# Ten weight parts of the memory's keys and values multiplied as rounded part and remainder instead of as native float32

## The chip, the cores and the metric

The kernel runs on one core of a Trainium2 chip. The metric is the device time of one execution in microseconds (us); the median of several runs is given. The engines are TensorE (PE, with its weight loads as PEld), VectorE (DVE), ScalarE (ACT), GpSimd (POOL) and SyncE (SP), which issues the transfers from memory.

## The reference

A trunk of two layers on 256 tokens of width 1024, all in float32. Each layer adds three things to the residual stream h: a mixer (an input projection of 2368 columns, two causal convolutions, a gated position mixing, a group norm, an output projection), a cross attention of 4 heads over 256 memory tokens, and a feed-forward part (a dense SwiGLU of 2816 in layer 0, eight experts of 3584 of which each token takes two in layer 1). A last norm follows. What the change touches is the projection of the normalized memory to keys and values:

```python
q = (xn @ w_xq).reshape(bsz, s, X_HEADS, X_HEAD_DIM)
k, v = jnp.split(memn @ w_xkv, 2, axis=-1)
scores = jnp.einsum("bshd,bmhd->bhsm", q, k) * (X_HEAD_DIM ** -0.5)
```

w_xkv is 1024 x 2048 in each layer, so keys and values of one layer are 16 parts of 128 x 1024 weights.

## The kernel before

**Parts and chunks.** All weights come through one stream of parts, 128 partitions x 1024 columns in most cases, loaded two at a time as a chunk of 1 MB by SP (L172) into a ring of 21 buffers (R_BUFS). In each layer the stream gives the mixer's input weights (wa, wb, wc), the key parts kb0 to kb7 (128 key columns each), the value parts vb0 to vb5 (two for each head of 256 columns, heads 0 to 2), eight parts of the mixer's output projection (mo), the value parts vb6 and vb7 of head 3, then q and the output of the attention. In layer 1, kb0 comes before the mixer's weights, kb1 has a chunk of its own behind them, and kb2 to kb5 are loaded and split during the dense feed-forward part and kept (L425 to L434).

**Two ways to multiply.** A part is either split or full. A split part is rounded to float32r by ACT (hi, L198), DVE subtracts that from the part (lo, L199), and each product becomes three rounded ones (mm3, L219 to L222): hi by hi, and each hi with the other side's lo. The other side must be split as well: for keys and values that is `ms`, which `split_m` (L468) makes from the normalized memory `mt`, its lo by DVE at L475. A full part is used as it lies, with `mt` itself, in one native float32 product: L463 for keys, L492 for values. The string FULL (L62) says for each of the sixteen parts of a layer which it is: eight keys, vb0 to vb5, then vb6 and vb7. In layer 1 the entries 0 and 1 go to kb0 and kb1 (L430), and 2 to 5 are not used, since those parts are kept (L425).

**What sets the order.** The program is written out by hand: each engine works through its instructions in the order in which the code issues them. `Stream.get` (L206) hands out the next part and, before that, splits parts up to three ahead (SPLIT_AHEAD), as long as they lie within three chunks of the current one (SPLIT_BUFS):

```python
while self.ns < min(i + 1 + ahead, len(self.parts)) and self.parts[self.ns][0] < c0 + bufs:
    self.do_split()
```

So a part's copy and subtraction are issued with the product of the part three places before it. `do_split` allocates hi and lo for a whole chunk when it first meets a part of it that is not full, and issues the loads three chunks ahead. Where the mixer stands is set by ORDER (L52), one string for each layer:

```python
ORDER = ["L 13 s b k a 4 k 5 k m 8 g 11 r k k 41 k 68 k 30 x t k 183 v1000 v8 33",
         "7 b s a k k k 4 m g 23 k k r k 42 k 86 v 31 t 14 v4 66"]
```

Here k is the next key part (`k_block`, L448), v the next head of values (`v_head`, L477), x is `split_m`, and a number is that many taps of the convolutions on DVE (`pop`, L142; the taps are at L548). In layer 1 `split_m` runs in the dense feed-forward part. The other letters are the branches: b transposes the second convolution back (L671, PE at L675, product at L677), s and a are the norm of the gated part (its last line L633), m the position mixing (PE at L687), g the gate (L697), r the scaling of the two branches (`sc_bc`, ending at L664), t their transposes (L300). With each part of wc, taps are issued as well, one in layer 0 and two in layer 1 (TAPS). Behind ORDER come the transposes of the first convolution (L724), its norm on DVE, head 2 of the values (L734), then the output projection. Evictions of keys and values are split too (L272 on ACT, L273 on DVE).

Of the kernel before, what the change touches and what calls it, by code (L numbers as in the profile page):

```python
# [58 lines left out]
ATTEND = ["q0 q1 S0 q2 S1 T0 q3 O0 T1 S2 S3 O1.T2.T3.O2.O3.",  # L59
          "q0 q1 S0 q2 T0 S1 q3 T1 O0 S2 S3 O1..T2 T3.O2 O3.."]  # L60

FULL = ["1111111110001100", "0110001111101100"]  # L62
SPL = [(j * 512, min(512, FF - j * 512)) for j in range((FF + 511) // 512)]


# [19 lines left out]
def trunk(tc, x, xt_in, mem, mt_in, wa, wb, wc, wl0, wk1, wl1, wff, wmoe, cc, tk, moec, ident_d, gfin, out):  # L85
    nc = tc.nc
    PE, ACT, DVE, POOL = nc.tensor, nc.scalar, nc.vector, nc.gpsimd
    with contextlib.ExitStack() as c:
# [1327 lines left out]
        def seq(a, n, w, full=None):  # L1416
            full = full or (False,) * (n * a.shape[0])
            return [(a[i], w, full[i * n:(i + 1) * n]) for i in range(a.shape[0])]

        def group(l):  # L1420
            return seq(wa[l], 2, 1024) + seq(wb[l], 2, 3 * BW) + seq(wc[l], 2, 2 * CW)

        def rest(l, a):

            f = tuple(x == "1" for x in FULL[l])
            n = l * KEPT
            f = f[2 * (l + n):14] + (False,) * 8 + f[14:16] + (False,) * 16
            return seq(a[n:], 2, 1024, f)

        one = (FULL[1][0] == "1",), (FULL[1][1] == "1",)  # L1430
        st = Stream(group(0) + rest(0, wl0) + seq(wff, 2, 1024) + seq(wk1[0:1], 1, 1024, one[0]) + group(1)
# [191 lines left out]
```

## Time and profile before

| | |
|---|---|
| median of 3 runs | 1512.85 us (1511.56 to 1518.7) |
| the profiled execution | 1510.55 us |
| its span on the core | 1508.7 us |
| mean granted TensorE clock | 0.989 |
| HBM over the span | 303 GB/s |

The span is the time from the first to the last instruction in the trace; the profiled execution's own time has what lies around it as well. A timeline row has the start, the time that the row takes, the engine, the line, the operation, out<-in and the count, and in brackets the idle time before it and what ended that. Rows that follow each other with one line and operation are merged. The start-to-start distance of matmuls tells their price better than the time of one, since they are pipelined.

### The profile page before, as it was taken

What the parts mean: (1) busy time and instruction counts of PE and PEld (TensorE: products, weight loads), DVE (VectorE), ACT (ScalarE), POOL (GpSimd) and SP (SyncE); (2) the same over time, 40 slices, a digit from 0 to 9 for tenths busy, and PEclk for the clock granted to TensorE, in tenths of its full rate; (3) what the DMA queues carried; (4) which work ended last, traced back from release to release, by engine and by line L of the source; (5) the groups of instructions that cost most, each with busy time, mean ns of one, the idle gap of its engine ahead of it and who ended that gap; (6) DMA issues with size and microseconds to landing.
All of it is one profiled execution on the core that took longest, in us unless ns stands there. A gap on an engine that the chain in (4) does not pass through costs nothing.

```text
span 1508.7 us, 20807 instructions
## 1 busy us (share of the span) xinstructions
PE 1469.5 (97%) x7757; PEld 1270.9 (84%) x7757; DVE 1293.9 (86%) x1496; ACT 1043.2 (69%) x1224; POOL 7.9 (1%) x23
## 2 busy tenths in 40 slices
PE   8999999999999998999999999999999999999995
PEld 7998988888999897788887878888888888888884
DVE  7988777545698866889999999999999999999996
ACT  7547565434544554688887788887878887888884
POOL 0000000000000001000000000000000000000000
PEclk9999999999999998899999999999999999999998
DMA  9535464544542547399999999999999999999992
GB/s 363 236 112 195 156 247 159 210 178 156 178 178 116 195 168 307 124 376 401 421 381 421 360 403 413 416 386 411 366 397 414 411 392 386 390 403 415 421 421 86
DMA packets 65326, 459.04 MB, mean 304 GB/s; under 512 B 7232, under 2 KB 7744, under 8 KB 11840
## 3 DMA queue, kind: packets, MB, share of 16 engines
q1 hardware_dynamic: 65216, 457.62, 76.5%
q8 instruction: 63, 1.03, 0.3%
q14 instruction: 47, 0.39, 0.1%
HBM read 456.55 MB, written 1.05 MB: 303 GB/s over the span
## 4 chain that ended last, share of the span: by engine, by line
PE 90%; DVE 4%; issue 2%; ACT 2%; DMA 1%; POOL 0%; SPq 0%; DVEq 0%; ACTq 0%; POOLq 0%
PE mm L1204 31%; PE acc L1204 16%; PE mm L220 5%; PE mm L222 5%; PE mm L221 5%; PE mm L1227 3%; PE acc L221 3%; PE acc L222 3%; PE acc L220 3%; PE mm L463 3%; PE z L221 2%; PE z L222 2%; PE z L220 2%; DVE lo L199 2%; PE mm L1149 2%
## 5 line engine op out<-in xcount | busy, mean ns | idle before, releaser
L199 DVE TENSOR_TENSOR lo<-w,hi 128x2048 fp32r<-128x2048 f32 (+3 forms) x504 | 946.4, 1917 | 56.9 <-ACT hi L198 37.8
L198 ACT ACTIVATE hi<-w 128x2048 fp32r<-128x2048 f32 (+3 forms) x504 | 795.1, 1619 | 111.9 <-PE mm L1204 58.0
L1204 PE MATMUL mm<-hi,xg 128*128 128x512 f32 x1344 | 405.4, 393 | 1.6 <-ACT xg L278 1.2
L1204 PEld LDWEIGHTS mm<-hi,xg 128*128 128x128 f32 x1344 | 253.0, 189 | 53.7 <-ACT xg L278 1.4
L1204 PE MATMUL mm<-lo,xg 128*128 128x512 f32 x896 | 295.3, 391 | 0.0
L1204 PE MATMUL acc<-hi,hl 128*128 128x512 f32 x672 | 217.4, 398 | 0.0
L1204 PEld LDWEIGHTS mm<-lo,xg 128*128 128x128 f32 x896 | 168.8, 188 | 34.1
L1204 PE MATMUL acc<-lo,hl 128*128 128x512 f32 x448 | 157.7, 393 | 0.0
L1204 PEld LDWEIGHTS acc<-hi,hl 128*128 128x128 f32 x672 | 125.2, 189 | 24.4
L1204 PEld LDWEIGHTS acc<-lo,hl 128*128 128x128 f32 x448 | 84.8, 189 | 17.4
L220 PE MATMUL z<-hi,xt 128*128 128x320 f32 (+1 forms) x256 | 79.0, 308 | 7.0 <-ACT xt L338 7.0
L221 PE MATMUL z<-lo,xt 128*128 128x320 f32 (+1 forms) x256 | 77.9, 304 | 0.2 <-DVE lo L199 0.2
L222 PE MATMUL z<-hi,xt 128*128 128x320 f32 (+1 forms) x256 | 78.0, 304 | 0.0
L548 DVE SCALAR_TENSOR_TENSOR ca<-ca,cct 128x256 f32<-128x256 f32 x180 | 77.1, 482 | 0.2
L220 PE MATMUL mm<-hi,xt 128*128 128x512 f32 (+1 forms) x192 | 71.9, 375 | 0.0
L222 PE MATMUL mm<-hi,xt 128*128 128x512 f32 (+1 forms) x192 | 71.5, 372 | 0.0
L221 PE MATMUL mm<-lo,xt 128*128 128x512 f32 (+1 forms) x192 | 71.4, 372 | 0.0
L1227 PEld LDWEIGHTS mm<-twice,gu 128*128 128x128 f32 x448 | 58.3, 191 | 6.0 <-ACT gu L1217 2.1
L1227 PE MATMUL mm<-twice,gu 128*128 128x64 f32 x448 | 56.2, 268 | 2.0 <-ACT gu L1217 2.0
L220 PEld LDWEIGHTS z<-hi,xt 128*128 128x128 f32 x256 | 49.7, 194 | 7.2 <-ACT xt L338 7.0
L221 PEld LDWEIGHTS z<-lo,xt 128*128 128x128 f32 x256 | 49.6, 194 | 0.5 <-DVE lo L199 0.5
L222 PEld LDWEIGHTS z<-hi,xt 128*128 128x128 f32 x256 | 49.5, 193 | 0.0
(284 smaller groups left out, 1891.5 us busy)
## 6 DMA issues: line engine op xcount, KB each, us to landing
w<-in_wmoe_dram SPq DMA_DIRECT2D x336, 1024.0 KB, 8.0
w<-in_wl_dram SPq DMA_DIRECT2D x39, 1024.0 KB, 4.8
w<-in_wff_dram SPq DMA_DIRECT2D x33, 1024.0 KB, 4.8
w<-in_wb_dram SPq DMA_DIRECT2D x8, 960.0 KB, 8.9
w<-in_wa_dram SPq DMA_DIRECT2D x5, 1024.0 KB, 4.9
w<-in_wc_dram SPq DMA_DIRECT2D x8, 640.0 KB, 4.6
tk<-in_tk_dram SPq DMA_DIRECT2D x2, 1024.0 KB, 10.5
mt<-in_mem_t_dram SPq DMA_DIRECT2D x2, 1024.0 KB, 8.2
```

Of the source, the lines that this page charges most:

```text
L198: ACT.activation(hi[:, ws], r, AF.Copy)
L199: DVE.tensor_tensor(lo[:, ws], r, hi[:, ws].bitcast(F32), op=OP.subtract)
L220: PE.matmul(ps, ah, bh, start=start, stop=False)
L221: PE.matmul(ps, ah, bl, start=False, stop=False)
L222: PE.matmul(ps, al, bh, start=False, stop=stop)
L463: PE.matmul(self.kps[:, d, :], w[:, ks], self.mt[:, k, :], start=k == 0, stop=k == KC - 1)
L548: return lambda: DVE.scalar_tensor_tensor(dst, src[:, k:k + S], w, dst, op0=OP.mult, op1=OP.add)
L1149: PE.matmul(ps[:, j * n:(j + 1) * n], src(t)[:, kk], self.pg[:, t, :], start=t == 0, stop=t == NT - 1)
L1204: PE.matmul(out, a, w, start=first and i == 0, stop=last and i == len(ops) - 1)
L1227: PE.matmul(ps[:, f * n:(f + 1) * n], w, twice, start=True, stop=True)
```

## The change

Ten entries of FULL go from 1 to 0. In layer 0 the parts kb7, vb0, vb4 and vb5, and in layer 1 kb7, vb0, vb1, vb2, vb4 and vb5, are split and multiplied with `ms` in three rounded products. kb0 to kb6 of layer 0, and kb1 and kb6 of layer 1, stay native. Nothing else changes.

```diff
-FULL = ["1111111110001100", "0110001111101100"]
+FULL = ["1111111000000000", "0110001000000000"]
```

## Rows read from the trace of the kernel before

**Rows 1.** The page, part 1: busy time of each engine.
```profile
PE 1469.5 (97%) x7757; PEld 1270.9 (84%) x7757; DVE 1293.9 (86%) x1496; ACT 1043.2 (69%) x1224; POOL 7.9 (1%) x23
```
**Rows 2.** Table of stretches: length, then busy us of PE, PEld, DVE, ACT, POOL.
```profile
470.00:480.00 10.00, 10.00 (x48) 8.80 (x48) 9.83 (x32) 1.54 (x2) 0.00 (x0) 1.00 0.26 92
```
**Rows 3.** Waits of PE, 62 to 545 us (all): total, times, longest.
```profile
PE acc L221 <- DVE lo L199: 0.2, 1, 0.2
```
**Rows 4.** Timeline of PE in layer 1, rounded products left out.
```profile
461.20 2.34 PE L687 MATMUL mm<-cv,tk 128*128 128x64 f32 x20
469.19 7.07 PE L463 MATMUL mm<-mt,w 128*128 128x256 f32 x32
476.09 7.07 PE L492 MATMUL mm<-w,mt 128*128 128x256 f32 x32
```
**Rows 5.** Lines L463 and L492, whole span: count, least, median, greatest ns.
```profile
L463 PE MATMUL mm<-mt,w x176: 377/380/484, 65.3 to 475.9; 128*128 128x256 f32 x176
L492 PE MATMUL mm<-w,mt x128: 377/380/382, 96.4 to 497.8; 128*128 128x256 f32 x128
```
**Rows 6.** Timeline of PE in layer 0: first and last of 48 rounded products.
```profile
102.70 0.28 PE L220 MATMUL mm<-hi,ms 128*128 128x256 f32 x1
...
108.34 0.28 PE L222 MATMUL mm<-hi,ms 128*128 128x256 f32 x1
```
**Rows 7.** Groups by line and shape, 60 to 150 us: busy us, mean ns.
```profile
L199 DVE TENSOR_TENSOR lo<-w,hi 128x1024 fp32r<-128x1024 f32 x16 | 19.0, 1221 | 1.1 <-ACT hi L198 1.1
L198 ACT ACTIVATE hi<-w 128x1024 fp32r<-128x1024 f32 x17 | 17.5, 1061 | 0.0
```
**Rows 8.** Timeline of DVE in layer 0.
```profile
90.39 0.69 DVE L273 TENSOR_TENSOR k<-mm,k 128x512 fp32r<-128x512 f32 x1
90.99 1.52 DVE L548 SCALAR_TENSOR_TENSOR ca<-ca,cct 128x256 f32<-128x256 f32 x3
...
93.03 1.22 DVE L199 TENSOR_TENSOR lo<-w,hi 128x1024 fp32r<-128x1024 f32 x1
94.16 2.35 DVE L475 TENSOR_TENSOR ms<-mt,ms 128x1024 fp32r<-128x1024 f32 x2
```
**Rows 9.** Timeline of PE in layer 0: the last key part.
```profile
92.92 3.62 PE L463 MATMUL mm<-mt,w 128*128 128x256 f32 x16
```
**Rows 10.** Timeline of DVE in layer 1.
```profile
444.94 0.88 DVE L548 SCALAR_TENSOR_TENSOR ca<-ca,cct 128x256 f32<-128x256 f32 x2
...
449.29 1.66 DVE L548 SCALAR_TENSOR_TENSOR ca<-ca,cct 128x256 f32<-128x256 f32 x4
451.43 1.07 DVE L677 TENSOR_TENSOR y<-mm,y 128x320 f32<-128x320 f32 x2 [0.47 <-PE mm L675]
...
459.98 0.49 DVE L633 TENSOR_TENSOR cv<-cv,tk 128x320 f32<-128x320 f32 x1
...
462.03 0.69 DVE L273 TENSOR_TENSOR k<-mm,k 128x512 fp32r<-128x512 f32 x1 [0.95 <-ACT k L272]
...
478.91 1.56 DVE L664 TENSOR_TENSOR y<-y,t 128x640 f32<-128x640 f32 x2
```
**Rows 11.** Line L172, 443.5 to 444.1 us: the issue and its landing.
```profile
L172 SPq DMA_DIRECT2D w<-in_wl_dram x1: 328/328/328, 443.8 to 443.8; - x1
...
DMA to landing us min/median/max: 4.9/4.9/4.9
```
**Rows 12.** Timeline of layer 0: the output projection's fifth part.
```profile
127.89 0.19 PEld L221 LDWEIGHTS acc<-lo,xt 128*128 128x128 f32 x1 [0.21 <-DVE lo L199]
```
**Rows 13.** Stretches (granted clock behind POOL), timeline of PE, waits of PE.
```profile
624.30:634.70 10.40, 10.40 (x43) 9.63 (x43) 6.74 (x12) 4.65 (x12) 0.00 (x0) 0.51 0.23 95
1484.50:1488.00 3.50, 3.50 (x10) 2.73 (x9) 3.07 (x3) 0.40 (x1) 0.00 (x0) 0.51 0.01 2
...
623.64 6.38 PE L1149 MATMUL mm<-pg,h 128*128 128x64 f32 x32 [3.14 <-DVE pg L1134]
...
PE mm L1179 <- DVE y L273: 4.5, 5, 1.2
```

## The prediction, made before the change was run

> **What bounds the kernel now.** I read the busy shares of the page first: TensorE (PE) is busy 97% of the span, VectorE (DVE) 86%, ScalarE (ACT) 69% [rows 1]. These are averages, and the ten weight parts are all used in two short stretches, the second half of the mixer of layer 0 (62 to 116 us) and of layer 1 (447 to 500 us). So the next view is the table of stretches, cut there. In 470 to 480 us PE is busy 10.00 of 10.00 us, but DVE is busy 9.83 and ACT only 1.54 [rows 2]. The reader is to see that PE has no gap, and that DVE, which would get new work, has no gap either. The waits of PE say the same from the other side: between 62 and 545 us PE waited once, 0.2 us, for a remainder that DVE writes at L199 [rows 3]. PE is the bound, with DVE a few microseconds behind it: whatever is taken off PE is worth its own time, and whatever is put on DVE ahead of something that PE needs is a wait that does not exist today.
>
> **What it takes off PE.** A native product leaves two records each: 11 parts of 8 products give the 176 records of L463, 8 parts the 128 of L492 [rows 5]. From 469.19 to 476.09 us PE went through 32 records, two parts, so a native part costs 3.45 us; the next 32 end with the same figure [rows 4]. The three rounded products at L220 to L222 start every 0.120 us: 48 of them from 102.70 to 108.34 us [rows 6]. A split part has 24, so 2.88 us. Each of the ten parts saves PE 0.57 us, 5.7 us in all. The Trainium skill (FP8 and Floating Point Precision, "TensorE Precision Notes") states that true FP32 takes 4 passes; were the three rounded products one pass each, an estimate from that would be a quarter of the part, 0.86 us, and 8.6 us for the ten (the sum below would come out 2 us lower). The rows show less, 0.57, and the rows decide.
>
> **What it adds.** Ten more copies at L198 on ACT, 1.06 us each, and ten more subtractions at L199 on DVE, 1.22 us each [rows 7] (1.13 from start to start, 93.03 to 94.16 us [rows 8]). ACT's 10.6 us I cost at nothing: it is the least busy engine in these stretches [rows 2]; were that cover gone, each copy would delay its subtraction by up to 1.06 us. No transfer is added. Five chunks that had no rounded tiles (in both layers the one with kb6 and kb7 and the one of head 2, in layer 1 the one of head 0) now take two buffers of the ring each, so later weight loads find a free buffer later. No row prices this: the lower end is nothing, since such loads were issued many microseconds ahead of use, the upper end some 5 us, the time of one load [rows 11]. I take nothing, as no wait of PE in rows 3 is for a load.
>
> The subtractions are issued three parts ahead and stand in DVE's queue in program order. So for each one I ask where in that queue it lands, and what PE needs next from behind it.
>
> **Layer 0, last key part (kb7).** Today it is multiplied with mt itself and begins at 92.92 us [rows 9]. Split, it needs ms, the remainder of the memory, which DVE writes at L475 from 94.16 us, 2.35 us for two halves [rows 8]. Today nothing needs ms before vb1. Now two new subtractions are queued ahead of it: kb7's after the first L273 (90.39 us), vb0's after the three taps at 90.99 us. The first half of ms then begins at 94.16 + 2 x 1.13 = 96.4 and ends near 97.6 us. PE can do one product at 92.92 and then stands until 97.6: a wait of 4.6 us. From then kb7 and vb0 save 0.57 each. Parts vb4 and vb5 (head 2) save 1.15 more, which I count as nothing: four output parts later PE already waits for a remainder, [0.21 <-DVE lo L199] at 127.89 us [rows 12], behind a chain of DVE that starts when the convolution is transposed and does not move with head 2. Layer 0: 4.6 - 1.15 = **+3.45 us**.
>
> **Layer 1, kb7.** Its subtraction is issued with the last part of wc. The load that brings it is issued at 443.8 us and lands 4.9 us later, at 448.7 [rows 11]; the copy takes 1.06, so DVE can subtract from 449.8 to 450.95. In DVE's queue the subtraction stands behind six of the fifteen taps that run from 444.94 us (two for each of the three parts before it); a tap takes 0.40 us, four of them 1.66 with the tail [rows 10], so DVE is there at about 447.3 and stands. The nine taps behind it now end at 450.95 + 9 x 0.40 = 454.5 instead of 450.95. The chain b, s, a that starts at L677 today at 451.43 [rows 10] starts 3.1 us later. PE works on kb1 to kb3 meanwhile and needs the end of that chain at L687, at 461.20 us [rows 4]; L633 ended at 460.47 [rows 10], 0.7 us earlier, so PE waits 3.1 - 0.7 = **2.4 us**.
>
> **Layer 1, vb0 and vb1.** vb0's subtraction is issued at kb1 and goes into DVE ahead of the taps and of r. vb1's is issued at kb6, and in the order string r stands before that, so it comes behind L664, which today ends at 478.91 + 1.56 = 480.5 [rows 10]. With the 3.1 us from kb7, 1.13 from vb0, and 0.95 of DVE's idle time (at 462.03 [rows 10]) used up, L664 ends at 483.7 and vb1's remainder is ready at 484.9. PE reaches head 0 at 476.09 [rows 4] + 2.4 - 0.57 = 477.9, does vb0 for the first token tile (12 products, 1.4 us) and needs vb1 at 479.4: a wait of **5.5 us**. What of L664's own reader, the transposes after head 0? They come after the wait and are ready. Savings that count: kb7, vb0, vb1, vb2, 2.3 us, and some 0.5 of head 2's 1.15, since in this layer the remainder four parts on has that much slack. Layer 1: 2.4 + 5.5 - 2.8 = **+5.1 us**.
>
> **The clock.** After a wait of 3.14 us for pg, PE began again at 623.64 and its granted clock was 0.51, the 1.2 GHz level, through 624.3 to 634.7 us; a shorter dip stands at 1484.5 to 1488.0 (0.51); behind the waits for y at L1179, the longest 1.2 us, I found no fall [rows 13]. Two new waits of 4.6 and 5.5 us are longer than 3.14, so I expect a fall behind each. What it costs is half of the low stretch: 1.7 us by the short one, 5.1 by the long one, none if the clock holds. I take 2.2, near the short one: as at 1484 us dense products follow at once, while after 623.64 us L1149's small ones did. Two falls: **+4.4 us**. The Trainium skill (TensorE: Matmul & The Clock Gate, "Why this matters for your kernels") likewise warns that idle gaps between bursts of matmuls return the array to half rate; the trace agrees with the 3.14 us gap, and this is the rule that speaks against the change.
>
> **Sum.** Waits 4.6 + 2.4 + 5.5 = 12.5, savings that count 4.0, clock 4.4: 12.9 us longer. From 545 us on the experts' stage keeps PE the bound, with its loads issued only as buffers come free, so I let all of it pass to the end. The profiled execution took 1510.55 us (span 1508.7), which makes 1523.5; the median of the runs, 1512.85, is 2.3 above it, so on the median 1525.8, given as **1526**. A measurement of this kernel tells some 0.5% (7.6 us) from no change.
>
> **Rivals.** (a) *Not slower.* The subtractions are ready in time and PE's saving stands: 4.0 to 5.7 us, 1507 to 1509. Its place is the remainder of ms in layer 0 and of vb1 in layer 1; it decides if DVE gets to them before 92.9 and 479.4 us. For it: rows 3, almost no wait today. Against it: DVE is at 9.83 of 10 us in front of the second point [rows 2], and rows 8 leave no gap before the first. Even the full 5.7 stays within 0.5%. Chance 0.12.
> (b) *One wait only*, because kb7's load in layer 1 or the place of vb1's subtraction is not as I read it. With layer 0 alone and one short dip it is 3.45 - 2.8 + 1.7 = 2.4, so 1515; with the 2.4 of L687 and 2 us at vb1 left, 6.8, so 1520. Chance 0.15.
> (c) *Both waits, the clock holds*: + 8.5, 1521. Against it stands the fall after 3.14 us. Chance 0.13.
> (d) *Long dips or late loads*: two dips of 5.1 and up to 5 us for a load that waits for the ring: 12.5 - 4.0 + 10.2 = 18.7, to 1532, and to 1537 with the load. Chance 0.15. That the lookahead turns out to split nothing new, so that nothing changes, gets 0.02, since L463 has 176 records today and must have 16 x 9 = 144.
> The forecast itself, both waits with short dips, has 0.43.
>
> **Range.** 1515 to 1534 takes in the forecast, (c), most of (b) and most of (d); left out are (a) and the far end of (d). Over 0.5% slower means above 1520.4: the forecast, (c), (d), 0.71 together. Within 0.5% are (a), (b) and nothing-changes: 0.29, of which I give 0.04 to over 0.5% faster, which needs more than the whole saving of PE.
>
> **What would show it.** L463 with 144 records (9 parts), L492 with none; L198 and L199 with 514 each. Step by step: PE waiting at L221 for ms (L475) near 93 us for 4 to 5 us; DVE waiting for hi (L198) near 447 us, L687 starting near 463.6; PE waiting for lo (L199) near 479 us for about 5 us; the granted clock below 1 behind the first and third. I am wrong if PE's gaps there stay under 1 us, if the waits are there but the clock is 1.00, or if the wait is for a load instead.

## The result and the profile after

The changed kernel takes **1531.71 us** (median of 6 runs, 1527.27 to 1532.82), beside 1514.59 us for six runs of the kernel before (1511.56 to 1518.7). The ratio is 1.0108, with a 95% interval of 1.0086 to 1.0131, so the kernel is slower by over 0.5%. The execution that was profiled took 1532.82 us (span 1531.0, mean granted clock 0.979), the highest of its six; that of before, 1510.55, lies below all six of its own. The two spans are 22.3 us apart, more than the medians (17.1), and that difference has to be explained too.

First the counts. From the page of the changed kernel, part 1, and then the groups of part 5 and the row of line L463 (they answer to [rows 1, 5]):

```profile
PE 1476.7 (96%) x7837; PEld 1279.5 (84%) x7837; DVE 1305.5 (85%) x1506; ACT 1053.4 (69%) x1234; POOL 7.9 (1%) x23
...
L199 DVE TENSOR_TENSOR lo<-w,hi 128x2048 fp32r<-128x2048 f32 (+3 forms) x514 | 958.4, 1903 | 63.3 <-ACT hi L198 44.8
L198 ACT ACTIVATE hi<-w 128x2048 fp32r<-128x2048 f32 (+3 forms) x514 | 804.7, 1607 | 119.3 <-PE mm L1204 56.7
...
L463 PE MATMUL mm<-mt,w x144: 377/379/483, 65.7 to 481.3; 128*128 128x256 f32 x144
```

L463 has 144 records and L492 none: the ten parts are split. DVE has 11.6 us more to do and ACT 10.2, about ten times the prices of [rows 7]. PE's busy time went up by 7.2 us although its work went down. The clock does that: at half speed the same product counts twice.

Next the waits of PE from 62 to 560 us, the view of [rows 3], where before there was one row of 0.2 us (columns: total, times, longest):

```profile
PE mm L221 <- DVE lo L199: 4.9, 1, 4.9
PE mm L221 <- DVE ms L475: 4.5, 1, 4.5
PE mm L675 <- DVE cb L548: 2.3, 1, 2.3
PE mm L300 <- DVE y L664: 0.5, 1, 0.5
PE acc L221 <- DVE lo L199: 0.4, 2, 0.2
```

Three new waits hold 11.7 us. The first to come in time is that for ms, in layer 0. PE's timeline of the changed kernel, the first product of kb7, the second behind the wait, the last, and the start of vb0:

```profile
93.21 0.36 PE L220 MATMUL mm<-ms,hi 128*128 128x256 f32 x1
98.08 0.58 PE L221 MATMUL mm<-ms,hi 128*128 128x256 f32 x1 [4.50 <-DVE ms L475]
...
102.94 0.41 PE L222 MATMUL mm<-ms,lo 128*128 128x256 f32 x1
103.15 0.41 PE L220 MATMUL mm<-hi,ms 128*128 128x256 f32 x1
```

And DVE's timeline of the same stretch, to hold against [rows 8]:

```profile
91.37 1.22 DVE L199 TENSOR_TENSOR lo<-w,hi 128x1024 fp32r<-128x1024 f32 x1
92.50 1.52 DVE L548 SCALAR_TENSOR_TENSOR ca<-ca,cct 128x256 f32<-128x256 f32 x3
93.94 1.22 DVE L199 TENSOR_TENSOR lo<-w,hi 128x1024 fp32r<-128x1024 f32 x1
95.07 0.69 DVE L273 TENSOR_TENSOR k<-mm,k 128x512 fp32r<-128x512 f32 x1
95.67 1.22 DVE L199 TENSOR_TENSOR lo<-w,hi 128x1024 fp32r<-128x1024 f32 x1
96.80 2.35 DVE L475 TENSOR_TENSOR ms<-mt,ms 128x1024 fp32r<-128x1024 f32 x2
```

Two subtractions that did not exist before (91.37 and 93.94) now stand ahead of ms, which begins at 96.80 instead of 94.16. DVE has no gap: it is late because it has more to do. kb7 on PE took 103.15 - 93.21 = 9.94 us. Its 24 products cost 2.88 [rows 6] and the wait 4.50, so 2.56 are left, and those are the clock: the products behind the wait start every 0.21 us (102.94 to 103.15), not every 0.120.

In layer 1 the load of kb7 comes first. DVE of the changed kernel, rows that answer to [rows 10]:

```profile
456.27 1.23 DVE L199 TENSOR_TENSOR lo<-w,hi 128x1024 fp32r<-128x1024 f32 x1 [2.51 <-ACT hi L198]
457.41 0.88 DVE L548 SCALAR_TENSOR_TENSOR ca<-ca,cct 128x256 f32<-128x256 f32 x2
458.20 1.26 DVE L548 SCALAR_TENSOR_TENSOR cb<-cb,cct 64x256 f32<-64x256 f32 x3
...
460.97 0.88 DVE L677 TENSOR_TENSOR y<-mm,y 128x320 f32<-128x320 f32 x2
...
488.21 1.56 DVE L664 TENSOR_TENSOR y<-y,t 128x640 f32<-128x640 f32 x2
489.69 1.22 DVE L199 TENSOR_TENSOR lo<-w,hi 128x1024 fp32r<-128x1024 f32 x1
```

DVE stood 2.51 us for the copy of a weight part that was still on its way, and the taps of cb at 458.20, queued behind that subtraction, were late. PE needs them at L675. PE's timeline in layer 1 has that wait, then L687 without one, then head 0:

```profile
459.61 1.19 PE L675 MATMUL mm<-ident,cb 128*128 128x128 f32 x6 [2.29 <-DVE cb L548]
...
470.03 2.34 PE L687 MATMUL mm<-cv,tk 128*128 128x64 f32 x20
...
484.34 0.28 PE L220 MATMUL mm<-hi,ms 128*128 128x256 f32 x1
...
490.96 0.58 PE L221 MATMUL mm<-lo,ms 128*128 128x256 f32 x1 [4.90 <-DVE lo L199]
...
497.46 1.25 PE L300 MATMUL mm<-ident,y 128*128 128x128 f32 x10
```

At 490.96 PE goes on when the remainder of vb1 is there, which DVE could only begin at 489.69, behind L664. The head took 497.46 - 484.34 = 13.12 us: 48 products at 0.120 are 5.76, the wait is 4.90, and 2.46 are the clock.

The table of stretches of the changed kernel says the same of the clock (the figure behind POOL; 1.00 is the 2.4 GHz level, 0.5 the 1.2 GHz one). The stretches are those behind the wait for ms, around the wait at L675, and behind the wait for vb1's remainder:

```profile
96.00:103.20 7.20, 5.12 (x24) 5.12 (x25) 6.25 (x9) 0.00 (x0) 0.00 (x0) 0.54 0.10 41
452.00:459.00 7.00, 5.33 (x37) 5.06 (x35) 4.49 (x11) 3.79 (x6) 0.00 (x0) 1.00 0.98 415
459.00:465.00 6.00, 5.39 (x29) 4.54 (x30) 5.86 (x22) 4.31 (x23) 0.00 (x0) 1.00 0.51 194
490.00:497.40 7.40, 6.44 (x35) 6.44 (x36) 5.79 (x7) 0.00 (x0) 0.00 (x0) 0.60 0.00 0
```

**Where the 22.3 us lie.** I follow landmarks through both traces; their rows in PE's timeline, two of the kernel before and one of the changed kernel (its L675 of layer 1 stands above):

```profile
450.81 1.16 PE L675 MATMUL mm<-ident,cb 128*128 128x128 f32 x6
...
587.53 0.96 PE L969 MATMUL mm<-mct,xf 128*128 128x8 f32 x8
```

```profile
601.44 0.96 PE L969 MATMUL mm<-mct,xf 128*128 128x8 f32 x8
```

The first L675 of layer 0, ahead of all that the change touches, starts at 64.23 us before and 64.60 after (0.4 of unequal start). L675 of layer 1 starts at 450.81 and 459.61; its wait of 2.29 taken off, layer 0 has cost 6.1 us. The first router product of layer 1 (L969) starts at 587.53 and 601.44, so from the first L675 to it ("the front" from here on) it was 523.3 us and is 536.8: **13.5 us more, 6.1 in layer 0 and 7.4 in layer 1**. Behind L969 the change touches nothing, yet the rest of the span takes 921.2 us before and 929.6 after. Those 8.4 us are a question for the experiments.

### The profile page after: what moved, and what is told of

The parts are those of the page before. It is cut to its first block, busy times and chain, and to the rows that moved or that the text cites. A ratio compares the mean times of both kernels' runs of the same rounds, so it can differ in the third digit from the quotient of the medians.

```text
span 1531.0 us, 20992 instructions
## 1 busy us (share of the span) xinstructions
PE 1476.7 (96%) x7837; PEld 1279.5 (84%) x7837; DVE 1305.5 (85%) x1506; ACT 1053.4 (69%) x1234; POOL 7.9 (1%) x23
## 4 chain that ended last, share of the span: by engine, by line
PE 84%; DVE 10%; issue 2%; ACT 2%; DMA 1%; POOL 0%; SPq 0%; DVEq 0%; ACTq 0%; POOLq 0%
PE mm L1204 30%; PE acc L1204 16%; PE mm L221 5%; PE mm L222 5%; PE mm L220 5%; DVE lo L199 3%; PE mm L1227 3%; PE acc L221 3%; PE acc L222 3%; PE acc L220 3%; DVE ca L548 2%; PE mm L1149 2%; PE z L221 2%; PE z L222 2%; PE z L220 2%
## 5 line engine op out<-in xcount | busy, mean ns | idle before, releaser
L199 DVE TENSOR_TENSOR lo<-w,hi 128x2048 fp32r<-128x2048 f32 (+3 forms) x514 | 958.4, 1903 | 63.3 <-ACT hi L198 44.8
L198 ACT ACTIVATE hi<-w 128x2048 fp32r<-128x2048 f32 (+3 forms) x514 | 804.7, 1607 | 119.3 <-PE mm L1204 56.7
```

Source lines behind the costliest of these rows:

```text
L198: ACT.activation(hi[:, ws], r, AF.Copy)
L199: DVE.tensor_tensor(lo[:, ws], r, hi[:, ws].bitcast(F32), op=OP.subtract)
```

## The experiments

My theory: three of the ten parts cost all of it, because DVE's queue delivers something too late: ms behind kb7 of layer 0, the taps of cb behind kb7 of layer 1 (whose load DVE stands for), and the remainder of vb1 of layer 1 behind L664. The clock falls behind the two long waits, and the other seven parts gain a little or nothing. Rivals: every part costs its share (of buffers, of loads, of DVE); or the clock alone costs it, by chance; or a better place in the order would have given the gain. All runs start from the changed kernel. The front is the profile's L969 less its first L675, 523.3 in the kernel before; the rest is the span less L969. Each ratio is against runs of the kernel before made alongside (14 of them for the first four rows, 18 for the next four); a row marked "one" is a single execution and has no ratio.

| run | median us (range) | ratio to before, 95% | front | rest |
|---|---|---|---|---|
| kb7 of layer 0 native | 1522.68 (1518.49 to 1525.26) | 1.0052 [1.0028, 1.0076] | 530.5 | 921.4 |
| vb1 of layer 1 native | 1526.56 (1522.44 to 1527.38) | 1.0080 [1.0056, 1.0104] | 532.0 | 923.5 |
| kb7 of layer 1 native | 1529.49 (1528.58 to 1531.02) | 1.0100 [1.0075, 1.0125] | 532.3 | 929.5 |
| all three native, seven split | 1514.38 (1511.61 to 1517.29) | 0.9991 [0.9974, 1.0008] | 521.7 | 923.6 |
| waits filled with products | 1524.84 (1520.7 to 1527.55) | 1.0056 [1.0037, 1.0075] | 534.9 | 926.5 |
| layer 0: ms earlier | 1527.32 (1524.35 to 1529.05) | 1.0067 [1.0046, 1.0088] | 532.9 | 929.2 |
| both orders changed | 1525.49 (1524.49 to 1527.46) | 1.0063 [1.0043, 1.0082] | 530.1 | 928.5 |
| both orders, kb7 of layer 1 native | 1520.3 (1514.83 to 1523.44) | 1.0025 [1.0011, 1.0040] | 527.6 | 920.3 |
| before, once more | 1516.09 (one) | | 523.2 | 925.8 |
| before, a third time | 1519.15 (one) | | 523.2 | 929.8 |
| changed kernel, once more | 1527.17 (one) | | 537.5 | 923.2 |
| only three split | 1509.41 (one) | | 521.6 | 921.1 |

**Which parts carry it.** Four kernels that give parts back:

```diff
-FULL = ["1111111000000000", "0110001000000000"]
+FULL = ["1111111100000000", "0110001000000000"]
```

> The changed kernel with one part put back: kb7 of layer 0 is native again, nine parts stay split. Theory (the cost is three waits of PE on DVE's queue and the clock that falls behind two of them): the 4.5 us wait for ms (L475) is gone, so is the half-speed stretch near 97 us (about 2.8 us), and 0.57 us of PE comes back; the first router product (L969, at 601.4 us in the changed kernel) starts about 6.7 us earlier, near 594.7; the waits at L675 and for vb1 in layer 1 stay at 2.3 and 4.9 us. Rival (the cost comes from the buffers and loads that every split part takes, in equal shares): L969 moves by a tenth of 13.9, 1.4 us. Rival (most of the difference is clock stretches of the experts' stage that come by chance): L969 hardly moves.

```diff
-FULL = ["1111111000000000", "0110001000000000"]
+FULL = ["1111111000000000", "0110001001000000"]
```

> The changed kernel with vb1 of layer 1 native again, nine parts split. Theory: the wait of 4.9 us for vb1's remainder (L199) behind L664 is gone and the half-speed stretch near 489 us (about 2.5 us) with it, against 0.57 us more of PE: L969 about 6.8 us earlier, near 594.6; the waits in layer 0 (4.5 us) and at L675 (2.3 us) stay. A smaller wait may come up at vb2's or vb3's remainder, which stand behind it in DVE's queue, under 1 us. Rival of equal shares: 1.4 us.

```diff
-FULL = ["1111111000000000", "0110001000000000"]
+FULL = ["1111111000000000", "0110001100000000"]
```

> The changed kernel with kb7 of layer 1 native again, nine parts split. Theory: DVE no longer stands for the load of kb7, so the 2.3 us wait of PE at L675 is gone; DVE's chain to L664 comes 3.1 us earlier and PE 2.4 - 0.57 us earlier, so the wait for vb1 stays, near 3.6 us, and the clock still falls behind it: L969 2 to 4 us earlier, near 598. Rival of equal shares: 1.4 us. Rival (the 2.3 us at L675 come from the taps alone, not from kb7's subtraction): the wait at L675 stays.

```diff
-FULL = ["1111111000000000", "0110001000000000"]
+FULL = ["1111111100000000", "0110001101000000"]
```

> The changed kernel with those three parts native again (kb7 of both layers, vb1 of layer 1), seven parts split. Theory: no wait of PE over 0.6 us between 62 and 560 us, no half-speed stretch before the router; L969 near the 587.5 us of the kernel before, less about 0.57 x 4 us that count of the seven, so 585 to 587.5, and the time the same as before or up to 2 us shorter. Rival of equal shares: seven tenths of the cost stay, L969 near 597.

Each native part took its own wait away and left the other two. With kb7 of layer 0 native the wait for ms is gone and the front is 6.3 us shorter than the 536.8 of the changed kernel; vb1 gives 4.8, kb7 of layer 1 4.5. The second had been expected some 2 us lower: behind the wait at L675, 2.17 us there, the clock now fell, which it had not done in the first profile of the changed kernel. Each gain is read from one profile and holds what the clock did in it, which differs by some 2 us between profiles (see the account of the clock below). The three gains add up to 15.6, and all three together gave 15.1; that they agree so closely is in part luck. What PE still waited for in that kernel, with seven parts split:

```profile
PE mm L300 <- DVE y L664: 0.5, 1, 0.5
PE acc L221 <- DVE lo L199: 0.4, 2, 0.2
```

Its front is 1.6 us *shorter* than before the change, and the time is that of before (0.9991). So seven of the ten parts cost nothing, nor do the buffers of the three chunks that take rounded tiles for them (the two chunks of kb6 and kb7 are all native again here): equal shares are refuted. The tables of stretches show how little room there is. First the kernel before, from L687 to L724, then the kernel with seven split parts in the same part of the work:

```profile
461.00:491.00 30.00, 30.00 (x192) 27.90 (x191) 24.87 (x63) 11.26 (x42) 0.00 (x0) 1.00 0.10 37
```

```profile
461.70:491.00 29.30, 29.30 (x212) 28.02 (x211) 29.09 (x68) 14.30 (x45) 0.00 (x0) 1.00 0.21 73
```

DVE's busy time (third figure with a count) goes from 24.87 of 30 us to 29.09 of 29.3. The four subtractions of vb0, vb2, vb4 and vb5 (1.13 us each) took the room that DVE had: some 0.2 us are left.

**How much of it is the clock.** The edit adds products that nobody reads, 38 ahead of kb7 in layer 0 and 41 ahead of vb1 in layer 1, so that PE works where it stood. Nothing is left out; the lines behind move by one to nine.

```diff
+                if self.l == 0 and i == KC - 1:
+                    z = mm("fill")
+                    for _ in range(FILL[0]):
+                        PE.matmul(z[:, 0:S], w[0][:, 0:P], self.ms.hi(0), start=True, stop=True)
...
+                        if self.l == 1 and hd == 0 and t == 0 and k == 4:
+                            z = mm("fill")
+                            for _ in range(FILL[1]):
+                                PE.matmul(z[:, 0:S], self.ms.hi(0, tok(0)), parts[0][0][:, 0:S], start=True, stop=True)
```

> The changed kernel, all ten parts split, with matmuls added whose results nobody reads: 38 of 128x256 ahead of kb7 in layer 0 and 41 between vb0 and vb1 in layer 1, 0.12 us each, on operands that are ready. They lie inside the two waits (4.5 and 4.9 us). Theory: DVE is as late as before, so the waits are filled, not shortened, and what is saved is the clock alone: no half-speed stretch near 97 and 489 us, L969 about 5.3 us earlier than in the changed kernel (601.4), near 596. Rival (the falls of the clock are not caused by PE standing still): the half-speed stretches stay and L969 stays at 601 or comes later.

The table of stretches of that kernel, behind the two filled waits and behind L684 (L675 in the other kernels):

```profile
97.00:104.00 7.00, 7.00 (x59) 6.86 (x58) 7.00 (x11) 2.49 (x3) 0.00 (x0) 1.00 0.30 101
457.00:464.00 7.00, 7.00 (x20) 5.07 (x20) 6.78 (x27) 3.52 (x22) 0.00 (x0) 0.53 0.34 135
490.00:498.00 8.00, 8.00 (x70) 8.00 (x69) 7.42 (x11) 2.48 (x7) 0.00 (x0) 1.00 0.17 51
```

Where PE was kept busy the clock stayed at 1.00, in both places: the 2.56 and 2.46 us belong to the idle time of PE. The remainders were hardly earlier for it (ms begins at 96.56 us and vb1's subtraction at 489.50; 96.80 and 489.69 in the changed kernel), so the waits' own time stayed, now filled with products. The front came out at 534.9 and not some 5 us below the changed kernel, because the clock fell at 457 us instead, behind a wait of 2.1 us that I had not filled. By the row above that fall cost some 3.3 us (7.00 us at 0.53). Of the 11.6 us by which this front is still longer than that of the kernel before, some 8 are then left with the clock at 1.00 behind both long waits: the rival that the clock alone makes the difference is refuted.

**Whether the order could be mended.** In layer 0 ms goes ahead of the two parts, at the price of later taps:

```diff
-ORDER = ["L 13 s b k a 4 k 5 k m 8 g 11 r k k 41 k 68 k 30 x t k 183 v1000 v8 33",
+ORDER = ["L 13 s b k a 4 k 5 k m 8 x g 2 r k k k k t k v1000 v8 33",
```

> The changed kernel, all ten parts split, with layer 0's order changed: the split of the memory (x) stands ahead of the gate (g), six taps ahead of r fewer, and the taps that are left come in the middle of head 0. Theory: the place in DVE's queue is what costs, not the amount of work: the wait for ms (4.5 us) and the half-speed stretch near 97 us are gone, with at most 1 us of new waits, L969 near 594.5. Layer 1 as in the changed kernel (waits of 2.3 and 4.9 us). Rival (DVE simply has too much to do in this stretch): the wait moves to the transposes of the first convolution (L724), which need all taps, and L969 stays within 2 us of 601.4.

The wait for ms and the fall behind it are gone, and kb7 and vb0 bring their saving: L724 of layer 0 starts 43.1 us after the first L675, before the change 44.2 (108.46 - 64.23). L969 still came 3.4 us later than expected (597.9 against 594.5). L300 waits 1.1 us for y instead of 0.5, and the wait for vb1's remainder is 0.5 us shorter than in the changed kernel; what is left is the price of a fall of the clock behind L675 of layer 1, which is seen in the 1.88 us of its row:

```profile
454.17 1.88 PE L675 MATMUL mm<-ident,cb 128*128 128x128 f32 x6 [2.12 <-DVE cb L548]
```

In layer 1 the next kernel moves r, the taps and head 0 as well, so that vb1's subtraction comes ahead of them:

```diff
-         "7 b s a k k k 4 m g 23 k k r k 42 k 86 v 31 t 14 v4 66"]
+         "7 b s a k k k m g 10 k k r k k v10 t v1000 66"]
```

> As the run before, with layer 1's order changed too: 10 taps ahead of r instead of 27, the rest in the middle of heads 0 and 1, all ten parts split. Theory: r and with it vb1's remainder come about 5 us earlier in DVE's queue, so the wait for vb1 falls from 4.9 us to under 1 and the half-speed stretch near 489 us goes; the 2.3 us at L675 stay; a wait of 1 to 3 us for the taps may come up at L724 of layer 1. L969 near 588, the time within 3 us of the kernel before. Rival (DVE has too much to do in layer 1): the 4.9 us come back at L724, L969 near 594.

Its row of L675 has the same wait ahead of it and takes 1.19 us, not 1.88: here the clock held.

```profile
454.28 1.19 PE L675 MATMUL mm<-ident,cb 128*128 128x128 f32 x6 [2.17 <-DVE cb L548]
```

Still the front was a miss, 530.1 us; L969 came at 595.1, near the 594 of the rival. Its waits of PE from 62 to 560 us:

```profile
PE mm L724 <- DVE ca L548: 4.8, 2, 3.4
PE mm L675 <- DVE cb L548: 2.2, 1, 2.2
PE mm L300 <- DVE y L664: 1.1, 1, 1.1
...
PE mm L221 <- DVE lo L199: 0.2, 1, 0.2
```

The wait for vb1's remainder shrank from 4.9 to 0.2 us, and L724 now waits 4.8 us for the taps that were put behind it. To see whether kb7's subtraction is what is too much, the next kernel has the same orders and kb7 of layer 1 native:

```diff
-FULL = ["1111111000000000", "0110001000000000"]
+FULL = ["1111111000000000", "0110001100000000"]
```

> As the run before, with kb7 of layer 1 native, nine parts split. Theory: the 2.3 us at L675 are gone as well, and no wait of PE over 1 us is left between 62 and 560 us; of the 9 x 0.57 us of PE some 3 to 4 us count, so L969 is at 584 to 586.5, 1 to 3.5 us ahead of the kernel before, and the time 0 to 4 us under it, hardly to be told from no change. Rival: a wait at L724 of 2 us or more, L969 at 587.5 or later.

A miss again, on the rival's side: L969 came at 592.9. The wait at L675 is gone, but PE's timeline at L724 shows:

```profile
490.11 0.27 PE L724 MATMUL mm<-ident,ca 128*128 128x128 f32 x1
493.60 0.47 PE L724 MATMUL mm<-ident,ca 128*128 128x128 f32 x1 [3.22 <-DVE ca L548]
495.56 1.11 PE L724 MATMUL mm<-ident,ca 128*128 128x128 f32 x4 [1.49 <-DVE ca L548]
```

and its table of stretches ahead of that:

```profile
476.00:486.00 10.00, 10.00 (x80) 9.81 (x79) 9.97 (x17) 5.03 (x10) 0.00 (x0) 1.00 0.13 43
486.00:496.00 10.00, 5.30 (x40) 4.78 (x39) 9.89 (x20) 2.38 (x3) 0.00 (x0) 0.81 0.43 169
```

DVE is busy 9.97 and 9.89 of 10 us up to its last tap. The order tried in layer 1, with kb7 and without, only chose which reader stands in front of DVE. In layer 0 there was room; that no order of layer 1 has room for vb1 is argued from these busy times and not shown. I did not try to give DVE's work to another engine.

**The rest of the span, and head 2.** Three kernels are unchanged ones, profiled again: the kernel before twice, the changed one once.

> The kernel before, unchanged, for one more profiled execution. Theory: the front's landmark (first router product, L969) stands near 587.5 us as before (within a us of start jitter), and half-speed stretches in the experts' stage (near 829, 1051 or 1272 us, behind gaps of about 1.5 us) come in some executions and not in others, whatever the kernel. Rival: the kernel before never has them, and they belong to the change.

> A second execution of the kernel before. Same expectations as for the first: L969 near 587.5 us; a stretch at half speed in the experts' stage would show that they come without the change (theory), none in either would leave the rival standing.

> The changed kernel, unchanged, once more. Theory: the two waits of 4.5 and 4.9 us and that of 2.3 us stand again, with half-speed stretches behind the first two, and L969 comes near 601 us (within 2); the stretches in the experts' stage may be two, one or none, and with none the execution is about 10 us shorter than the profiled one before it. Rival: the same two stretches again near 844 and 1070 us.

The fourth also makes head 2's four parts native, so that only vb0 of layer 0 and vb0 and vb2 of layer 1 stay split:

```diff
-FULL = ["1111111000000000", "0110001000000000"]
+FULL = ["1111111100001100", "0110001101001100"]
```

> The three costly parts native as in the run that kept seven split, and head 2's four parts (two in each layer) native too; three of the ten stay split. Theory: what head 2's split parts save on TensorE is lost at the wait that follows them (L300 for y), so L969 counted from the first L675 stays within a us of the 521.7 of the run with seven split. Rival: the saving counts in full, four times 0.57 us, and L969 comes 2.3 us later, at 524.0.

The front repeats closely: 523.3, 523.2 and 523.2 us in the three executions of the kernel before, 536.8 and 537.5 in the two of the changed one. The rest does not: 921.2, 925.8 and 929.8 before, 929.6 and 923.2 after. PE's timeline of the second execution of the kernel before, at two gathers of one line in the experts' stage, shows why:

```profile
828.58 5.32 PE L1149 MATMUL mm<-pg,hs 128*128 128x64 f32 x32 [1.46 <-DVE pg L1134]
...
1277.72 3.79 PE L1149 MATMUL mm<-pg,hs 128*128 128x64 f32 x32 [1.46 <-DVE pg L1134]
```

The same 32 products behind the same gap of 1.46 us take 5.32 us once and 3.79 us once; in 830 to 838 us the granted clock of that execution is 0.57. In the changed kernel's first profile they took 5.50 and 6.36 us at 842 and 1069 us, behind gaps of 1.47, and in the first profile of the kernel before 3.79 each time. So falls behind these gaps come without the change, and the first profile of before happened to have none there (its fall near 624 us, behind the longer gap [rows 13], stands in every profile). The 8.4 of the 22.3 us between the two profiles need no change to come about. That the change makes them likelier is not shown (means of the rest 925.6 and 926.4 us), nor excluded by five executions.

With head 2 native PE's list of waits is that of [rows 3] again:

```profile
PE acc L221 <- DVE lo L199: 0.2, 1, 0.2
```

and the front stays at 521.6 us, beside 521.7 with head 2 split. Its four parts save nothing that lasts. The three that are left save 523.3 - 521.6 = 1.7 us, which is three times 0.57. The front of this kernel is the shortest found, by 0.1 us. Its one time, 1509.41 us beside 1511.57 for the kernel before, does not prove a gain: 1.7 us are 0.1%.

## Why the prediction was right

The forecast was slower, 1526, within 1515 to 1534, by late remainders in two places with the clock behind them, and by a late load in layer 1. That is what happened. Its steps, with the front of the first profiles as the measure:

| step | predicted us | measured us |
|---|---|---|
| layer 0: wait of kb7 for ms | 4.6 | 4.50 |
| layer 0: clock behind it | 2.2 | 2.56 |
| layer 0: saving of kb7 and vb0 | -1.15 | -1.15 (L724 in the run with ms earlier) |
| layer 0: head 2 | 0 | 0.2 (layer 0's L724 to layer 1's L675) |
| layer 1: delay by kb7's load | 2.4, at L687 | 2.29, at L675 |
| layer 1: wait for vb1's remainder | 5.5 | 4.90 |
| layer 1: clock behind it | 2.2 | 2.46 |
| layer 1: saving of kb7, vb0, vb1, vb2 | -2.3 | -2.3 (L675 to L724) |
| layer 1: head 2 | -0.5 | 0 |
| front | +12.9 | +13.5 (+14.2 the second time) |

That the sums lie 0.6 us apart is in part luck: vb1's wait was taken 0.6 us too long, while the two falls came out 0.6 dearer and head 2 0.7 worse than predicted. ACT's copies, costed at nothing, cost next to nothing: from 62 to 560 us DVE waited 13.3 us for copies instead of 10.5, and 2.51 of the 2.8 more is kb7's load.

**kb7 of layer 1** had its size right and its place wrong. The load was issued at 450.17 us, 6.4 later than before as layer 0 was longer, landed 4.92 later, and DVE stood 2.5 us, just as worked out. But I followed the delayed taps only to L677 on DVE and from there to L687. Three of them are taps of cb, and PE itself reads cb at L675, one step earlier. PE stood there for 2.29 us. As that moved PE as a whole, the chain on DVE, 3.0 us later than layer 0 alone explains, cost it nothing more at L687. That both paths give 2.3 to 2.4 is luck. The kernel with this part native shows that L675 was the place: that wait alone went.

**vb1** was sized 0.6 us too high: L664 came 2.8 us later than layer 0 alone makes it, not 3.2, and PE did one product more before it stood.

**The clock** cost 2.56 and 2.46 us in the first profile of the changed kernel, where I had 2.2. The second shows that a fall has no fixed price: kb7 of layer 0 took 9.09 us there (93.33 to 102.42), which less 2.88 and a wait of 4.48 leaves 1.73, and head 0 of layer 1 took 13.10 (485.06 to 498.16), which less 5.76 and 4.41 leaves 2.93. Over the nine falls behind these two waits in all profiles it was 1.6 to 2.9, 2.1 in the mean, so 2.2 was a fair middle. I had chosen between 1.7 and 5.1 by the nearer row, and that held; whether the dense products are the reason was not tested. Rival (c), that the clock holds, is refuted by the two stretches at half speed, and rival (d), that a fall costs 5.1 us each, by the 2.56 and 2.46. No wait of PE between 62 and 560 us names a load, so its other half falls too.

**Head 2** in layer 1 gave nothing, where I had counted 0.5. In layer 0 the place is near the one predicted: with seven parts split, the transposes at L300 four output parts later wait 0.5 us for y, beside the 0.2 for a remainder that was there before. (The row at 127.89 us that I read as PE's wait is one of its weight loads, PEld; PE's own 0.2 us come at 132.48.) In layer 1 the saving is there at L300 (with seven parts split it starts 441.9 us after the first L675, with head 2 native 442.9) and all but gone at the next transposes, L318, 11 us later (452.6 and 452.5). In between, with seven parts split, the weight loads stand 0.27 us for y and 0.45 and 0.61 for remainders, with head 2 native 0.18 once: the slack of 0.5 that I had counted on is not there.

**Rival (a)** is what the kernel with the three parts native shows: where the remainders are in time, PE's saving stands, here 1.6 us. Rival (b), one wait only, is refuted by the list of waits.

**What the prediction missed** is the rest of the span. The 1526 lies 5.7 us below 1531.71; 1.7 of that is the kernel before itself, whose median over six runs is 1514.59 and not 1512.85. I let the front's loss pass to the end unchanged, and that is right as far as the runs can tell. But I measured from one profiled execution whose rest was among the shortest seen (920.3 to 929.8 us over fourteen profiles). The 3.9 us between the predicted 13.2 (1526 less 1512.85) and the measured difference of medians, 17.1, are 0.6 of the front and, for the remainder, no more than six runs of each kernel can tell apart when the rest varies by 9.5.

Of the saving per part: the Trainium skill (FP8 and Floating Point Precision, "TensorE Precision Notes") gives 4 passes to true FP32, and from that I had estimated 0.86 us; the 1.7 us of the three parts left are 0.57 each, as the rows of before have it.

## What to carry to other kernels

A cheaper form of a product is only worth its price on TensorE if the operand that it needs in addition is ready. Here 0.57 us were to be gained per part, and the three parts whose subtraction came late in DVE's queue or held it up lost eight to eleven times that (6.3, 4.8 and 4.5 us came back with them native). Look at the queue of the engine that prepares the operand just ahead of each single use, part by part: of ten parts that look alike, three decided, and the list of waits told which. Where DVE was busy 29.1 of 29.3 us, the reordering tried moved a wait to another reader and did not remove it; and when a delayed item is followed along its queue, every reader of everything behind it must be asked for, not only the chain one has in mind.

## What the runs showed of the hardware that I had not expected

The clock does not follow from the length of a wait alone. Behind the waits of 3.9 to 4.9 us at the two places it fell every time, nine times of nine. Behind the wait of 2.1 to 2.3 us at L675 it fell in five profiles (the second of the changed kernel, those with kb7 of layer 0 or vb1 of layer 1 native, with the waits filled, and with ms earlier) and held in two (the first of the changed kernel, and both orders changed), with the same instructions ahead of it in both profiles of the changed kernel. Behind the gaps of 1.47 us at L1149 it fell in some executions of one kernel and held in others. The Trainium skill (TensorE: Matmul & The Clock Gate, "What's actually happening") says that the number of slow matmuls differs from run to run of the same kernel; the products near 829 us agree, with 3.79 us in the first execution of the kernel before and 5.32 in the second.

The trace of the kernel before already had a sign of it, which the prediction did not use. The short dip at 1484.5 us [rows 13], from which it priced a fall, stands behind a wait of only 1.97 us:

```profile
1483.17 1.11 PE L1227 MATMUL mm<-twice,gu 128*128 128x64 f32 x8 [1.97 <-ACT gu L1217]
```

So the predicted wait of 2.4 us in layer 1, which was given no fall, should have had a chance of one. For a forecast this means that a wait of 1.5 to 2.5 us should carry a second price that may or may not come, here some 1.7 to 3.4 us for a fall behind L675. Three times I left it out, in the expectations for vb1 native, for the filled waits and for the earlier ms, and they came out 2.2 to 3.4 us too low.
